# A table's copies queued behind a weight load instead of behind a write of activations (one-core decoder trunk)

## The chip, the cores and the metric

One core of a Trainium2 chip runs the whole program. The metric is device time in microseconds (us) of one execution, as the median of several.

## The reference

Two layers work on 256 tokens of width 1024. Each layer mixes tokens (short convolution, sliding-window attention, chunked spatial gating) and then runs PEER, a retrieval over 16384 single-neuron experts. All the parts that matter here are in PEER:

```python
q = (t @ w_pq).reshape(T, PEER_HEADS, 2, PEER_HALF)
s = jnp.einsum('thpk,hpnk->thpn', q, sub_keys)
top_s, top_i = lax.top_k(s, PEER_TOPK)                 # 16 of 128 keys, twice per head
...                                                    # best 16 of the 256 pairs
gate = jax.nn.softmax(best_s, axis=-1)
u = expert_down[experts]
act = jax.nn.gelu(jnp.einsum('td,thkd->thk', t, u), approximate=False)
vv = expert_up[experts]
return jnp.einsum('thk,thkd->td', gate * act, vv)
```

Besides, each layer needs 48 columns of modulation, `silu(c) @ w_ada + b_ada`.

## The kernel before, in words

The kernel computes PEER densely: all 16384 activations for all 256 tokens, in 128 chunks of 128 experts (the **down stage**, function `experts`), each multiplied by its gate (zero for experts that a token didn't choose), and then all of the up projection (the **up stage**, function `combine`). One part of the up projection is done sparsely instead: for the second 128 tokens and the last `WIDE[layer]` output columns (256 in layer 0, 384 in layer 1) the chosen rows alone are fetched and added.

For that the down stage builds a table in the chip's memory, `rows[layer]` (L100), one row for each expert. A row has `WIDE` columns of the up matrix and 128 columns with that expert's ungated activations of the second 128 tokens. `act` (L944) fills it, once for each pair of chunks: ScalarE (ACT) computes the ungated activations (L949) into the tile `ungated`, of which there is one buffer, and sends it (L950) from its own queue; SyncE (SP) copies the up matrix's columns from memory to memory (L951, 256 KB a pair in layer 0, 384 KB in layer 1). The activations' piece has 129 columns and begins one column early, at `WIDE - 1`, in the last column that the copy writes too. So the copy, which stands second in the text, has to wait until the piece has landed, and then sets that column right. In the up stage, GpSimd fetches 128 sets of rows by index (L1007) and VectorE adds them (L1013, L1018).

The other work of the down stage: each chunk of weights (128 by 1024, 512 KB) is loaded by SP into one of five `raw` buffers (`dma_ahead`, L170; the load is L175), at most five chunks ahead of the chunk that is split next (`cast_step`, L207). ACT makes its rounded half `hi` (L232), VectorE (DVE) the rest `lo` (L225); TensorE (PE) then does three products for each of eight slices (L303 to L305) into a `ch` bank, of which there are two, each for a pair of chunks. ACT applies the gelu (L959, L962) and the ungated gelu (L949). From about the middle on, PE also makes gates from one-hot tiles (L918 to L932), which DVE and ACT multiply in (L939, L942).

In layer 0 the stream of loads in the down stage is mixed with 40 chunks of `w_ada` (`mix`, L291). These don't go to PE: DVE reduces each of them by itself with two instructions (L193), and then the buffer is free. Layer 1's down stage has none of them.

The order of instructions on each engine outside the stretches marked as manual (the up stage and the two bridges are manual) is set by a planner that follows an estimate of each instruction's time (`schedule_with_timeline_sim=True`, L1244). Each engine and each queue then runs its instructions in that order; an instruction that waits holds up those behind it.

Of the kernel before, what the change touches and what calls it, by code (L numbers as in the profile page):

```python
# [9 lines left out]
F32 = mybir.dt.float32  # L10
# [3 lines left out]
AF = mybir.ActivationFunctionType  # L14
# [3 lines left out]
P = 128  # L18
# [3 lines left out]
D = 1024  # L22
# [22 lines left out]
WIDE = (256, 384)  # L45
# [13 lines left out]
def hybrid_trunk(ctx: ExitStack, tc: tile.TileContext, x_in, c_in, vec_in, w_ada, w_in, w_out, w_pq,  # L59
                 keys, down, up, rel_bias, sgu_w, sgu_b, out):  # L60
    nc = tc.nc
    consts = ctx.enter_context(tc.tile_pool(name="consts", bufs=1))
    stream = ctx.enter_context(tc.tile_pool(name="stream", bufs=1))
    work = ctx.enter_context(tc.tile_pool(name="work", bufs=1))
# [35 lines left out]
    rows = {n: dram.tile([P * P, WIDE[n] + P], F32, name=f"rows{n}") for n in range(DEPTH) if SPARSE[n]}  # L100
# [62 lines left out]
    class Src:  # L163
        c = cact
# [149 lines left out]
    def bank(tag, bufs):  # L314
        return psum.tile([P, 512], F32, name=tag, tag=tag, bufs=bufs)
# [590 lines left out]
    def experts(layer, rest):  # L906
# [37 lines left out]
        def act(pair, ps, tdone):  # L944
            tmp = gelu(pair, ps, tdone)
            if SPARSE[layer]:
                i = 2 * pair
                ungated = work.tile([P, 2, P + 1], F32, name="ungated", tag="ungated", bufs=1)
                nc.scalar.activation(ungated, ps.rearrange("p (i t) -> p i t", i=2)[:, :, P - 1:], AF.Gelu)  # L949
                nc.scalar.dma_start(rows[layer].rearrange("(j i) c -> i j c", i=P)[:, i:i + 2, WIDE[layer] - 1:], ungated)  # L950
                nc.sync.dma_start(rows[layer][i * P:(i + 2) * P, :WIDE[layer]],  # L951
                                  up[layer, i:i + 2, :, D - WIDE[layer]:].rearrange("j i c -> (j i) c"))
            return tmp

        def gelu(pair, ps, tdone):
            i = 2 * pair
            v = ps.rearrange("p (i t) -> p i t", i=2)
            if tdone < S:
                nc.scalar.activation(arena[:, i:i + 2, tdone:], v[:, :, tdone:], AF.Gelu)  # L959
            if tdone:  # L960
                tmp = work.tile([P, 2, S], F32, name="gt", tag="gt", bufs=1)
                nc.scalar.activation(tmp[:, :, :tdone], v[:, :, :tdone], AF.Gelu)  # L962
                return tmp
            return None
# [148 lines left out]
        for i in range(128):  # L1113
            pair, j = divmod(i, 2)
            if j == 0:
                ps = bank("ch", 2)
# [28 lines left out]
            if j == 1:  # L1145
                tdone = 4 * gdone
                pend = (pair, act(pair, ps, tdone), tdone)
# [101 lines left out]
```

## Time and profile before

| | us |
|---|---|
| median of 3 runs | 1821.18 |
| lowest and highest run | 1818.62, 1821.8 |
| the profiled execution, its own time | 1817.31 |
| its span, first to last instruction | 1815.6 |

One execution is profiled. Busy times are by engine; "PEld" is TensorE's weight load, "SPq" and "ACTq" are the queues in which SyncE and ScalarE issue transfers. A wait names the instruction that was released, what released it, the total in us, how often, and the longest. An instruction's row ends with the idle time of its engine ahead of it and what ended that, in square brackets.

### The profile page before, as it was taken

Reading aid. Unit: us, or ns where it says so; the run is one execution under the profiler, and the core shown is the slowest. Engines: PE = TensorE matmul, PEld = TensorE weight load, DVE = VectorE, ACT = ScalarE, POOL = GpSimd, SP = SyncE. Lnnn points to the kernel's source line nnn. Section 1 sums busy time; section 2 is a strip of 40 time slices with the busy share of each in tenths; the row PEclk is TensorE's granted clock in tenths of the full one; section 3 lists DMA queues with packets and bytes.
Section 4 is the critical chain, followed back from the end, with each engine's and each line's share of the span. In section 5 each row is a group of like instructions: output and inputs, shape, how many; then the busy total and the mean of one; then the engine's idle time right before and its main releaser. Section 6 shows DMA issues by size and latency. Waiting matters only on the chain. (4 is left out here: it accounts for less than half of the span.)

```text
span 1815.6 us, 34513 instructions
## 1 busy us (share of the span) xinstructions
PE 1746.4 (96%) x12504; PEld 1608.5 (89%) x12504; DVE 1517.4 (84%) x3465; ACT 915.4 (50%) x1419; POOL 921.3 (51%) x826
## 2 busy tenths in 40 slices
PE   7999998999999999999999999999999999999998
PEld 6789998998889988888889999999999998888886
DVE  5868988888888789999996689957778877999998
ACT  2445454454444554445456665555555546444543
POOL 1000102577889456666720002037999982777672
PEclk9999999999999999999999999999999999999999
DMA  9965687887787699999974456888787778999995
GB/s 369 323 232 165 228 276 262 285 264 257 255 260 243 228 317 329 338 337 343 342 258 152 139 175 191 269 269 274 250 257 225 248 240 292 361 346 343 358 350 206
DMA packets 189868, 492.97 MB, mean 272 GB/s; under 512 B 19521, under 2 KB 85441, under 8 KB 188546
## 3 DMA queue, kind: packets, MB, share of 16 engines
q1 hardware_dynamic: 134752, 405.33, 66.7%
q0 software_dynamic: 19984, 68.44, 10.2%
q10 hardware_dynamic: 34962, 17.01, 3.3%
q8 instruction: 98, 1.61, 0.4%
q14 instruction: 72, 0.59, 0.1%
HBM read 470.64 MB, written 62.00 MB: 293 GB/s over the span
## 5 line engine op out<-in xcount | busy, mean ns | idle before, releaser
L232 ACT CAST hi<-raw 128x1024 fp32r<-128x1024 f32 x538 | 563.9, 1050 | 609.7 <-PE ch L305 250.6
L225 DVE TENSOR_TENSOR lo<-raw,hi 128x1024 fp32r<-128x1024 f32 x538 | 660.1, 1229 | 124.2 <-ACT hi L232 120.1
L304 PE MATMUL ch<-hh,lo 128*128 128x256 f32 x2336 | 659.1, 282 | 17.3 <-DVE lo L225 17.1
L303 PE MATMUL ch<-hh,hi 128*128 128x256 f32 x2336 | 664.0, 284 | 3.1 <-ACT ungated L949 3.1
L305 PE MATMUL ch<-hh,hi 128*128 128x256 f32 x2336 | 655.3, 281 | 0.0
L918 POOL TENSOR_SCALAR oh<-iota,picks 128x128 f16<-128x128 f16 x512 | 509.8, 1013 | 236.4 <-DVE picks L848 127.2
L1007 POOL DMA_INDIRECT arena<-rows,arena x256 | 371.0, 1449 | 222.7 <-DVE arena L1018 103.4
L304 PEld LDWEIGHTS ch<-hh,lo 128*128 128x128 f32 x2336 | 444.8, 190 | 22.4 <-DVE lo L225 22.1
L303 PEld LDWEIGHTS ch<-hh,hi 128*128 128x128 f32 x2336 | 444.5, 190 | 4.2 <-ACT ungated L949 3.7
L305 PEld LDWEIGHTS ch<-hh,hi 128*128 128x128 f32 x2336 | 444.5, 190 | 0.0
L1027 PE MATMUL acc<-hi,hh 128*128 128x512 f32 (+2 forms) x1920 | 419.6, 359 | 3.8 <-DVE hh L985 2.6
L1027 PEld LDWEIGHTS acc<-hi,hh 128*128 128x128 f32 x1920 | 339.3, 188 | 50.5 <-DVE hh L985 7.0
L1027 PE MATMUL acc<-lo,hh 128*128 128x512 f32 x960 | 231.1, 361 | 3.3 <-DVE lo L225 2.8
L1027 PEld LDWEIGHTS acc<-lo,hh 128*128 128x128 f32 x960 | 172.5, 188 | 28.6 <-DVE lo L225 4.8
L1018 DVE SCALAR_TENSOR_TENSOR arena<-arena 128x256 f32<-128x256 f32 (+1 forms) x254 | 140.3, 552 | 9.1
L942 ACT ACTIVATE arena<-g 128x240 f32<-128x240 f32 (+35 forms) x128 | 41.6, 325 | 120.7 <-DVE arena L939 105.6
L779 POOL CAST arena<-arena 128x512 f16<-128x512 uint32 x32 | 27.2, 864 | 147.6 <-DVE arena L768 116.4
L923 DVE TENSOR_TENSOR oh<-oh,parts 128x512 f16<-128x512 f16 x256 | 101.4, 437 | 0.0
L193 DVE SCALAR_TENSOR_TENSOR raw<-raw,acc 128x512 f32<-128x512 f32 x80 | 51.9, 684 | 54.2 <-DMA raw<-in_w_ada 54.2
L931 PE MATMUL g<-oh 128*128 128x128 f16 x512 | 75.8, 222 | 17.5 <-POOL oh L918 8.8
L1013 DVE SCALAR_TENSOR_TENSOR arena<-arena,chosen,ident 128x128 f32<-128x128 f32 x256 | 89.2, 349 | 1.7 <-DMA arena<-rows,arena 1.7
L921 DVE TENSOR_TENSOR oh<-iota,parts 128x512 f16<-128x512 f16 x128 | 56.7, 444 | 28.8 <-POOL oh L918 16.0
(231 smaller groups left out, 1788.7 us busy)
## 6 DMA issues: line engine op xcount, KB each, us to landing
raw<-in_down SPq DMA_DIRECT2D x256, 512.0 KB
raw<-in_up SPq DMA_DIRECT2D x256, 512.0 KB
raw<-in_w_ada SPq DMA_DIRECT2D x96, 512.0 KB
rows<-in_up SPq DMA_DIRECT2D x64, 384.0 KB
rows<-ungated ACTq DMA_DIRECT2D x128, 129.0 KB
raw<-in_w_pq SPq DMA_DIRECT2D x32, 512.0 KB
rows<-in_up SPq DMA_DIRECT2D x64, 256.0 KB
raw<-in_w_in SPq DMA_DIRECT2D x26, 512.0 KB
```

The source lines that it names most:

```text
L225: nc.vector.tensor_sub(lo, raw, hi.bitcast(F32))
L232: nc.scalar.copy(hi, raw)
L303: nc.tensor.matmul(dst, hi[:, cols], k[0], start=start, stop=False, **kw)
L304: nc.tensor.matmul(dst, lo[:, cols], k[0], start=False, stop=False, **kw)
L305: nc.tensor.matmul(dst, hi[:, cols], k[1], start=False, stop=stop, **kw)
L918: nc.gpsimd.tensor_scalar(oh[:, i, :], iota, picks[:, t:t + 1], None, op0=OP.is_equal)
L923: nc.vector.tensor_tensor(og[j], on, wide(1 + j), op=OP.mult)
L931: nc.tensor.matmul(dst, oh[:, i, :], og[0][:, i // 2, :, i % 2], start=True, stop=False)
L1007: nc.gpsimd.indirect_dma_start(out=ring[:, k % RING, :], out_offset=None, in_=rows[layer][:, :], in_offset=bass.IndirectOffsetOnAxis(ap=wh ...
L1013: nc.vector.scalar_tensor_tensor(v[:, wide:], v[:, wide:], chosen[:, 1, k:k + 1], ident, op0=OP.mult, op1=OP.mult, accum_out=w8[:, k:k + 1])
L1018: nc.vector.scalar_tensor_tensor(total, v[:, :wide], w8[:, k:k + 1], total, op0=OP.mult, op1=OP.add)
L1027: nc.tensor.matmul(acc[piece][:, :hi - lo], w[:, t * P:(t + 1) * P], u[:, lo:hi], start=piece not in opened, stop=last, skip_group_check=True)
```

## The change

The activations' piece loses the shared column: it has 128 columns and begins at `WIDE`. The copy then touches no column that another transfer writes. Without that wait the planner would be free to put it anywhere; the new call pins it, in SP's order of issue alone, behind the instruction last traced on SP, which is a load of weights (L175). It doesn't wait for that load to land.

```diff
@@ -945,11 +945,12 @@
             tmp = gelu(pair, ps, tdone)
             if SPARSE[layer]:
                 i = 2 * pair
-                ungated = work.tile([P, 2, P + 1], F32, name="ungated", tag="ungated", bufs=1)
-                nc.scalar.activation(ungated, ps.rearrange("p (i t) -> p i t", i=2)[:, :, P - 1:], AF.Gelu)
-                nc.scalar.dma_start(rows[layer].rearrange("(j i) c -> i j c", i=P)[:, i:i + 2, WIDE[layer] - 1:], ungated)
-                nc.sync.dma_start(rows[layer][i * P:(i + 2) * P, :WIDE[layer]],
-                                  up[layer, i:i + 2, :, D - WIDE[layer]:].rearrange("j i c -> (j i) c"))
+                ungated = work.tile([P, 2, P], F32, name="ungated", tag="ungated", bufs=1)
+                nc.scalar.activation(ungated, ps.rearrange("p (i t) -> p i t", i=2)[:, :, P:], AF.Gelu)
+                nc.scalar.dma_start(rows[layer].rearrange("(j i) c -> i j c", i=P)[:, i:i + 2, WIDE[layer]:], ungated)
+                tc.keep_in_program_order(nc.sync.dma_start(
+                    rows[layer][i * P:(i + 2) * P, :WIDE[layer]],
+                    up[layer, i:i + 2, :, D - WIDE[layer]:].rearrange("j i c -> (j i) c")))
             return tmp
```

## Rows read from the trace of the kernel before

**Rows 1.** The page, its first lines: the span and the busiest engine.

```profile
span 1815.6 us, 34513 instructions
PE 1746.4 (96%) x12504; PEld 1608.5 (89%) x12504; DVE 1517.4 (84%) x3465; ACT 915.4 (50%) x1419; POOL 921.3 (51%) x826
```

**Rows 2.** Table by stretch: the two down stages, then two stretches of low clock.

```profile
core 0: us, PE busy (x) PEld busy (x) DVE busy (x) ACT busy (x) POOL busy (x), PEclk, DMA share, GB/s
195.00:632.00 437.00, 406.09 (x3554) 395.09 (x3553) 361.36 (x860) 212.91 (x374) 250.48 (x264) 0.98 0.79 258
1110.00:1508.00 398.00, 390.60 (x3563) 384.07 (x3563) 316.54 (x690) 214.22 (x375) 271.99 (x264) 1.00 0.80 250
275.20:278.60 3.40, 3.40 (x18) 3.40 (x18) 3.13 (x10) 0.98 (x1) 0.00 (x0) 0.50 0.91 269
323.00:326.40 3.40, 3.40 (x18) 3.40 (x17) 3.40 (x7) 1.43 (x2) 0.00 (x0) 0.50 0.70 206
...
```

**Rows 3.** Waits of SP's queue, stretch 195 to 632 us, then 1110 to 1508 us.

```profile
SPq L951 <- DMA rows<-ungated: 150.8, 54, 8.0
...
SPq L951 <- DMA rows<-ungated: 224.2, 63, 6.1
```

**Rows 4.** Waits of DVE, ACT and PE in layer 0's down stage, 195 to 632 us.

```profile
DVE raw L193 <- DMA raw<-in_w_ada: 54.2, 28, 4.9
...
ACT hi L232 <- DMA raw<-in_down: 14.0, 4, 5.0
ACT ungated L949 <- DMA rows<-ungated: 8.2, 9, 2.6
...
PE ch L304 <- DVE lo L225: 14.9, 16, 2.1
PE g L931 <- DVE oh L923: 7.2, 5, 2.1
```

**Rows 5.** Waits of ACT in layer 1's down stage, 1110 to 1508 us.

```profile
ACT hi L232 <- PE ch L305: 128.1, 97, 3.4
ACT ungated L949 <- DMA rows<-ungated: 30.0, 17, 3.2
```

**Rows 6.** Instructions in order, PE, 264 to 344 us: where it stood.

```profile
267.09 0.39 PE L303 MATMUL ch<-hh,hi 128*128 128x256 f32 x1 [0.97 <-ACT ungated L949]
274.92 0.39 PE L304 MATMUL ch<-hh,lo 128*128 128x256 f32 x1 [2.10 <-DVE lo L225]
283.31 0.39 PE L304 MATMUL ch<-hh,lo 128*128 128x256 f32 x1 [0.84 <-DVE lo L225]
321.73 0.38 PE L304 MATMUL ch<-hh,lo 128*128 128x256 f32 x1 [1.87 <-DVE lo L225]
337.96 0.22 PE L931 MATMUL g<-oh 128*128 128x128 f16 x1 [0.44 <-POOL oh L918]
```

**Rows 7.** Instructions in order, SP's queue, 260 to 276 us, and DVE's at 272 us.

```profile
264.57 0.50 SPq L951 DMA_DIRECT2D rows<-in_up  x1
265.12 0.60 SPq L175 DMA_DIRECT2D raw<-in_w_ada  x1
...
272.42 0.69 DVE L193 SCALAR_TENSOR_TENSOR raw<-raw,acc 128x512 f32<-128x512 f32 x1 [4.33 <-DMA raw<-in_w_ada]
```

**Rows 8.** Instructions in order, SP, ACT and DVE, 411 to 419 us.

```profile
411.07 0.33 SPq L175 DMA_DIRECT2D raw<-in_w_ada  x1
412.95 0.33 SPq L175 DMA_DIRECT2D raw<-in_down  x1
417.45 0.50 SPq L951 DMA_DIRECT2D rows<-in_up  x1
...
412.11 0.37 ACTq L950 DMA_DIRECT2D rows<-ungated  x1
...
416.48 0.69 DVE L193 SCALAR_TENSOR_TENSOR raw<-raw,acc 128x512 f32<-128x512 f32 x1 [3.33 <-DMA raw<-in_w_ada]
```

**Rows 9.** Instructions of line L949: count, least, median and most ns.

```profile
L949 ACT ACTIVATE ungated<-ch x128: 374/388/407, 195.6 to 1506.2; 128x258 f32<-128x258 f32 x128
```

**Rows 10.** The page, DMA queues of SP and ACT: packets, MB, share of 16 engines.

```profile
q1 hardware_dynamic: 134752, 405.33, 66.7%
q10 hardware_dynamic: 34962, 17.01, 3.3%
```

**Rows 11.** ACT's longest stop for the piece in layer 1, and that stretch's table.

```profile
1182.61 0.39 ACT L949 ACTIVATE ungated<-ch 128x258 f32<-128x258 f32 x1 [3.17 <-DMA rows<-ungated]
...
1162.00:1190.00 28.00, 28.00 (x247) 27.91 (x246) 23.76 (x47) 14.13 (x22) 3.60 (x2) 1.00 0.85 263
```

## The prediction

> **What bounds the kernel now.** I read the page's busy line first [rows 1]: PE is busy for 1746.4 of 1815.6 us, so at most 69 us of the span is time in which PE stands, wherever it lies. The change touches the two down stages, so the table by stretch comes next [rows 2]. Both stages do the same products (3554 and 3563 matmuls), but layer 0 takes 437.00 us and layer 1 takes 398.00. In layer 0 PE stands 437.00 - 406.09 = 30.9 us and has a granted clock of 0.98, which costs another 437 x 0.02 = 8.7 us. In layer 1 it stands 7.4 us at full clock. So this change can give at most about 40 us in layer 0 and 7 us in layer 1.
>
> Then the waits. SP stands at the copy for the activations' piece to land: 150.8 us in layer 0 and 224.2 us in layer 1, some 3 us for each copy [rows 3]. That is the wait that goes. What it is worth has to be read from those who wait for the loads behind it. In layer 1 ACT's list has no wait for a load at all [rows 5]: 224 us of SP's standing cost PE nothing there, because five buffers cover it. In layer 0 DVE waits 54.2 us in 28 pieces for `w_ada` chunks, ACT 14.0 us in 4 pieces for expert chunks [rows 4], and PE's own waits are for DVE (`lo` and the one-hots), which are queued behind those reductions.
>
> So the question is which of layer 0's late loads are late because of the copy. Two samples show both kinds. In the first [rows 7] the copy goes at 264.57 and the `w_ada` load right behind it at 265.12; DVE then waits 4.33 us and PE 2.10 us, after which its granted clock is 0.50 (1.2 of 2.4 GHz) for 3.4 us [rows 2, 6]. In the second [rows 8] the load goes at 411.07, ahead of the copy (417.45); DVE nevertheless reaches its reduction 2.1 us after the issue, and waits 3.33 us until 416.48. There the planner put the reduction too early for a load that takes 5.4 us; the copy has no part in it.
>
> **The change, part by part.**
>
> *SP's wait is gone.* Nothing else on SP replaces it: a copy then costs its issue only. The loads behind it (one or two in each pair) go when a buffer is free. Of layer 0's PE stops, five belong to loads issued behind a copy that had stood: 0.97 + 2.10 + 0.84 + 1.87 + 0.44 = 6.2 us [rows 6]. Two of them were followed by a spell at half clock of 3.4 us, which costs 1.7 us each [rows 2]: 3.4 us more. The sum is 9.6 us. I don't take all of it, since where the copy's delay goes, the other kind of wait remains: DVE waits 54.2 / 28 = 1.9 us for each of them on average, against 4.33 us in the sample. I take two thirds, 6.4 us. The lower bound of this term is 0 and the upper bound layer 0's whole 40 us (all `w_ada` waits gone); the five stops are the nearest rows.
>
> *Layer 1:* between 0 and the 7.4 us that PE stands. PE has no wait on a load there, so I take 0.
>
> *One column less on ACT:* 256 instead of 258 elements in an instruction of 388 ns [rows 9], 128 times. At 388 / 258 = 1.5 ns for each element at most that is 3 ns x 128 = 0.4 us of an engine that is busy half of the time. It is hidden by PE; without that cover it would be 0.4 us.
>
> *The activations' write, 129 to 128 columns:* ACT's queue takes 3.3% of the DMA engines, 0.033 x 1815.6 / 128 = 0.47 us for each piece [rows 10]. Starting on another column may make it cheaper or dearer; no row shows it. I bound it by -0.47 and +0.47 us of a landing of 5.3 us (412.11 to 417.45, [rows 8]) and take 0: ACT waits for that landing, PE doesn't.
>
> *The copies go earlier,* by the 3 us that they stood. They are pinned behind the load last traced, so they move past no load, and the bytes are the same. SP's queue took 0.667 x 1815.6 = 1211 us for 405 MB [rows 10], 3.0 us per MB; a copy is 0.78 us of all engines in layer 0, 1.17 us in layer 1. What it now meets is the activations' piece, which it used to follow. That is a rival below. POOL's first fetch of rows needs all copies; they land earlier than before, so nothing waits longer.
>
> *A new plan.* The planner sees other times, so the order on DVE and ACT in both down stages will differ in places. No row shows its price. The nearest bound is what the present order costs where no `w_ada` interferes, layer 1's 7.4 us; I take 0 and keep -4 and +5 us for the range.
>
> The sum: 1817.3 - 6.4 = 1810.9 us for the profiled execution. That one lies 3.9 us below the median of the runs shown, 1821.2; against the median it is 1814.8 us. A measurement of this kernel can tell about 0.2%, 3.6 us, from no change.
>
> **The rivals.**
>
> *No change (0.28).* Layer 0's waits are those of rows 8, made by the order on DVE: a reduction stands about 2 us behind its load's issue, and the load takes 5 us or more, with or without a copy. When the five stops shrink, DVE reaches the next reduction earlier and waits there instead. For it: 28 waits, far more than five, and layer 1, where SP's standing is worth nothing. Against it: the waits of over 4 us have a copy just ahead. The time is 1821 us. It would also be the outcome if the change did not do what it says and SP still stood at the copy for something else.
>
> A rule of the Trainium skill points the same way. "DMA: Bandwidth & Descriptors", section "Issuing engines are not separate DMA queues", says (in my words) that transfers issued by different engines share the same 16 DMA engines, and that an issuing queue of one's own saves only the time of issuing. By that rule, freeing SP alone gives no transfer time back, and the sum would be 0; the trace has it so in layer 1.
>
> *Slower (0.20): the copy gets in the way of the activations' piece.* Until now the copy was issued only when the piece had landed; now the copy's bytes are in the engines when the piece is sent. The piece lands later by up to the copy's 0.78 or 1.17 us. Its tile has one buffer, so ACT stands at the next L949, and behind that in its queue are the casts that PE needs. ACT already waits 17 times, 30.0 us in all, in layer 1 [rows 5]. The place where it decides: ACT stood 3.17 us and PE was busy 28.00 of 28.00 us around it [rows 11], so a stop of some 3 us is still covered. Beyond that each us reaches PE. If all 17 waits went over by 1.17 us, that would be 20 us, and 9 x 0.78 = 7 us in layer 0. Half of the sum is likelier, as the waits are of different length: +13, less the 6.4 gained, +7 us, 1828 us.
>
> On this another rule of that page of the Trainium skill speaks against the change: its section "Queues, rings and completion order", has a transfer's completion signal land only after every earlier write of the same DMA engine, across queues. The row agrees so far as 0.47 us of data takes 5.3 us to be reported [rows 8, 10].
>
> *A large gain (0.10).* If loads that go without delay are also spread more evenly, each takes less than 5.4 us, and half of the 54.2 us that DVE waits goes [rows 4], with it half of layer 0's 40 us: -20 us, 1801 us. Against it: DMA is at 0.79 in this stage anyway.
>
> **How the numbers follow.** The forecast, 5 to 12 us faster, has a chance of 0.42; no change 0.28, slower 0.20, large gain 0.10. Faster by over 0.2%: 0.42 + 0.10 = 0.52; within 0.2%: 0.28; slower: 0.20. The range goes from the large gain's near half, 1803, to the slower rival's 1828; what lies outside is about half of each of these two, 0.15. The likeliest case alone has 1809 to 1817.
>
> **What would show it.** Right: no row of SP's line for the copy waiting for the piece; layer 0's stretch shorter than 437 us by 5 to 10, with fewer and shorter waits for loads (below 54.2 and 14.0 us) and fewer spells at half clock; layer 1's stretch within 2 us. The rival "no change" shows as the same 50 us of DVE waiting for `w_ada` in spite of a free SP. The slower rival shows as ACT's waits for the piece well above 30.0 us in layer 1, with PE waiting for `hi` or L949. The forecast is wrong if PE's standing in layer 0 stays at 31 us, or if the new order brings PE a stop that stands in no row here.

## The result, and the profile after

| | before, us | after, us |
|---|---|---|
| median (4 runs each) | 1819.9 | 1802.61 |
| lowest and highest | 1814.51, 1821.8 | 1801.73, 1804.13 |
| the profiled execution, its own time | 1817.31 | 1804.13 |
| its span | 1815.6 | 1802.4 |

The ratio is 0.9911, 95% interval 0.9887 to 0.9934: 0.9% faster, or 16 us of 1819.9, where 6.4 us were forecast. The likeliest case was right in sign and too small; the median stands 0.4 us under the low end of the range (1803).

The first view is the table by stretch of the kernel after, cut as in [rows 2] (from 0.6 us ahead of the first ungated gelu of layer 0 to 3.8 us behind the first product of the up stage, and in layer 1 from 1.0 us ahead to 4.7 us behind); then a spell at half clock around PE's longest stop (3.53 us), and 3.4 us that follow its longest but one (2.30 us).

```profile
core 0: us, PE busy (x) PEld busy (x) DVE busy (x) ACT busy (x) POOL busy (x), PEclk, DMA share, GB/s
196.20:623.90 427.70, 399.51 (x3553) 388.22 (x3552) 362.43 (x864) 212.15 (x374) 239.64 (x264) 0.99 0.83 266
1099.40:1495.80 396.40, 389.08 (x3564) 383.27 (x3563) 317.86 (x698) 213.28 (x375) 270.81 (x264) 1.00 0.82 255
299.20:306.00 6.80, 5.95 (x28) 5.95 (x29) 6.38 (x16) 2.27 (x4) 0.11 (x1) 0.50 0.81 248
389.00:392.40 3.40, 3.40 (x34) 3.26 (x34) 3.40 (x8) 1.86 (x4) 2.15 (x1) 1.00 0.80 246
```

Layer 0's stretch went from 437.0 to 427.7 us, layer 1's from 398.0 to 396.4. In layer 0 PE stands 427.70 - 399.51 = 28.2 us against 30.9, so only 2.7 us of the 9.3 are standing. The other 6.6 us are PE's busy time, 406.09 to 399.51 for the same products, mostly because less of it ran at the lower clock (0.99 granted for the stretch against 0.98). These are two single executions; how far they stand for the kernels is taken up below.

The waits of layer 0's stretch answer to [rows 3, 4]: SP's queue, then DVE, ACT and PE.

```profile
SPq L175 <- DVE lo L225: 138.6, 65, 3.7
SPq L175 <- DMA raw<-in_w_ada: 48.3, 26, 3.7
```

```profile
DVE raw L193 <- DMA raw<-in_w_ada: 47.8, 30, 4.2
...
ACT ungated L949 <- DMA rows<-ungated: 20.3, 16, 3.7
...
PE ch L304 <- DVE lo L225: 13.7, 14, 2.3
PE ch L303 <- ACT ungated L949: 5.8, 3, 3.5
...
PE g L931 <- DVE oh L923: 3.8, 5, 1.1
```

SP no longer waits for the piece; it waits for buffers. ACT's 14.0 us of waits for expert chunks are gone. But DVE's waits for `w_ada` are almost what they were: 47.8 us in 30 pieces, against 54.2 in 28. One of them, in the order of time on SP's queue, DVE and PE:

```profile
379.45 0.33 SPq L175 DMA_DIRECT2D raw<-in_w_ada  x1
380.59 0.33 SPq L175 DMA_DIRECT2D raw<-in_down  x1
380.97 0.51 SPq L951 DMA_DIRECT2D rows<-in_up  x1
...
384.96 0.69 DVE L193 SCALAR_TENSOR_TENSOR raw<-raw,acc 128x512 f32<-128x512 f32 x1 [4.23 <-DMA raw<-in_w_ada]
...
388.74 0.38 PE L304 MATMUL ch<-hh,lo 128*128 128x256 f32 x1 [2.30 <-DVE lo L225]
```

The copy now stands right behind a load and holds nothing up. DVE came to its reduction 1.3 us after the load's issue and waited until 384.96, 5.5 us after it. PE paid 2.30 us. This is the pattern of [rows 8], and the change leaves it alone. Both samples are from the low end. By the timelines of SP and DVE, DVE reaches the 40 reductions of this stage 3.9 us (median) behind their loads' issue before the change and 4.1 us after it, which is still less than the 5.1 us (median) that a `w_ada` load takes to land.

### The profile page after: what moved, and what is told of

Read it like the earlier page. It is cut to its first block, busy times and chain, and to the rows that moved or that the text cites. A ratio compares the mean times of both kernels' runs of the same rounds, so it can differ in the third digit from the quotient of the medians.

```text
span 1802.4 us, 34404 instructions
## 1 busy us (share of the span) xinstructions
PE 1736.8 (96%) x12504; PEld 1599.5 (89%) x12504; DVE 1515.8 (84%) x3465; ACT 913.6 (51%) x1419; POOL 907.5 (50%) x826
## 3 DMA queue, kind: packets, MB, share of 16 engines
q1 hardware_dynamic: 134752, 405.33, 67.4%
## 5 line engine op out<-in xcount | busy, mean ns | idle before, releaser
L918 POOL TENSOR_SCALAR oh<-iota,picks 128x128 f16<-128x128 f16 x512 | 498.4, 991 | 235.4 <-DVE arena L833 67.4
L1028 PE MATMUL acc<-hi,hh 128*128 128x512 f32 (+2 forms) x1920 | 419.5, 359 | 2.8 <-DVE hh L986 2.4
L193 DVE SCALAR_TENSOR_TENSOR raw<-raw,acc 128x512 f32<-128x512 f32 x80 | 51.8, 683 | 47.8 <-DMA raw<-in_w_ada 47.8
```

The costliest lines, as they stand in the source:

```text
L918: nc.gpsimd.tensor_scalar(oh[:, i, :], iota, picks[:, t:t + 1], None, op0=OP.is_equal)
L1028: nc.tensor.matmul(acc[piece][:, :hi - lo], w[:, t * P:(t + 1) * P], u[:, lo:hi], start=piece not in opened, stop=last, skip_group_check=True)
```

## The experiments

All ratios are to the kernel before, run on the same chip. "Layer 0" is the stretch cut as above, in the one profiled execution; "stands" is that stretch less PE's busy time, "clock" its granted clock.

| kernel | ratio, 95% interval | layer 0, us | PE stands, us | clock |
|---|---|---|---|---|
| before | 1 | 437.0 | 30.9 | 0.98 |
| before_again | 0.9986 (0.9965 to 1.0006) | 438.8 | 31.2 | 0.97 |
| wait_kept | 0.9976 (0.9954 to 0.9999) | 429.7 | 31.0 | 0.99 |
| free_layer1 | 0.9974 (0.9954 to 0.9994) | 429.3 | 28.5 | 0.99 |
| free_layer0 | 0.9936 (0.9910 to 0.9961) | 419.3 | 24.5 | 1.00 |
| after | 0.9911 (0.9887 to 0.9934) | 427.7 | 28.2 | 0.99 |
| after_again | 0.9894 (0.9859 to 0.9930) | 428.7 | 31.8 | 1.00 |
| order_only | 0.9914 (0.9881 to 0.9946) | 419.5 | 23.4 | 0.99 |
| no_pin | 1.0483 (1.0455 to 1.0511) | 410.6 | 17.5 | 1.00 |
| before_no_ada | 1.0027 (1.0013 to 1.0041) | 398.3 | 6.5 | 1.00 |
| after_no_ada | 1.0006 (0.9993 to 1.0020) | 394.0 | 6.9 | 1.00 |
| before_reduce_late | 0.9892 (0.9867 to 0.9917) | 416.6 | 20.1 | 0.98 |
| after_reduce_late | 0.9799 (0.9770 to 0.9827) | 400.1 | 10.0 | 1.00 |
| order_reduce_late | 0.9794 (0.9775 to 0.9814) | 399.5 | 9.6 | 1.00 |

**The two kernels again.**

> The kernel before, a second time, for the spread. All theories: a ratio of 1.000. If the profile repeats, layer 0's down stage (from the first ungated gelu to the first product of the up stage) is 433 us again, layer 1's 392 us, and layer 0's has some six spells at half clock and 31 us in which PE stands. If a second profile differs by several us in a stage, so much of the 13 us between the two profiles is spread and not the change.

> The changed kernel, a second time. A ratio of 0.991 again (0.989 to 0.993). Layer 0's down stage 423 us against 433, half of the spells at half clock (three), PE standing some 28 us. If the spells are chance, this profile may have five or six and layer 0's stage is then nearer to 428 us.

Both ratios repeat. The profiles repeat in length (438.8 and 428.7 us), and here PE's standing hardly differs: 31.2 and 31.8 us. What differs is PE's busy time, 407.6 against 396.9 us, with a granted clock of 0.97 against 1.00. But neither execution is a typical one. That of after_again is the slowest of its six (1807.4 us, median 1798.2), and that of before_again has the lowest granted clock of its twelve (0.991 over the whole run, median 0.995). So this pair alone doesn't show that the gain is time at the lower clock.

**The wait kept, the column gone.** The wait for the landing stays by an explicit dependency instead of the shared column. In both down stages the orders on SP, ACT, DVE and PE are those of before.

```diff
-                tc.keep_in_program_order(nc.sync.dma_start(rows[layer][i * P:(i + 2) * P, :WIDE[layer]], ...))
+                copy = nc.sync.dma_start(rows[layer][i * P:(i + 2) * P, :WIDE[layer]], ...)
+                tc.add_manual_dep(copy.ins, piece.ins.name,
+                                  mybir.DependencyInfo(mybir.DependencyClass.Sync, mybir.DependencyReason.DATA))
```

> The shared column goes as in the change, but SP's wait for the piece stays, by an explicit dependency. Theory (SP's wait while the program runs is what cost): the time of the kernel before, ratio 1.000, SP stands some 375 us at the copy again. Rival (the piece of 128 columns, starting where the copy ends, is cheaper to write and lands sooner): ratio 0.991 as after the change, and a landing well below 5 us. Rival (the planner's order): its order of SP's queue is almost that of before, so 1.000 too.

0.9976, where 1.000 was expected: about a quarter of the gain, from the narrower piece alone. By itself this is barely clear of the spread (the kernel before came out at 0.9986 the second time), but two more comparisons below have the same 0.2 to 0.3%. Waits of SP in layer 0 and layer 1, as in [rows 3]:

```profile
SPq L951 <- DMA rows<-ungated: 130.4, 54, 6.1
...
SPq L951 <- DMA rows<-ungated: 202.3, 63, 6.1
```

SP stands 332.7 us instead of 375.0, some 0.3 us less for each copy: the piece lands that much sooner. The rest of the gain needs SP's wait to go. This profiled execution (1807.8 us) is one of the kernel's faster ones (median 1812.2), so its 429.7 us flatters it.

**The order kept, the wait gone.** The same edit with a dependency of order alone (`DependencyClass.NoSync`): the copy stands behind the piece's issue in the plan and waits for nothing of it.

> The copy is planned behind the issue of the piece, as an order alone: no wait for the landing. Theory (SP's wait is what cost): close to the changed kernel, ratio 0.990 to 0.994, with SP hardly standing at the copy. Rival (the gain is this particular new order of the work on DVE, ACT and PE): the order here is again a different one, so the ratio may be anywhere from 0.990 to 1.005, and DVE's waits for w_ada differ from the 48 us of after.

0.9914, the changed kernel's ratio, with quite another order on PE and DVE, and SP no longer stands at the copy. So the gain goes with SP's wait and not with one particular plan. No run has the order of before without the wait, so a share of the new orders isn't excluded; but two orders that differ this much give the same ratio.

**One layer at a time.** The pin in one layer, the explicit wait in the other (`if layer == 0`, or 1).

> The change in layer 0 alone; in layer 1 the copy waits for the piece as before. Theory (the late loads matter where w_ada is reduced): nearly the whole gain, ratio 0.988 to 0.993, with SP standing some 210 us at the copy in layer 1 for nothing. Rival (each layer gives its part, since SP stands 150 us in one and 215 in the other): ratio 0.995 to 0.996.

> The change in layer 1 alone; in layer 0 the copy waits for the piece. Theory: next to nothing beyond the kernel with the wait kept in both layers (0.998), ratio 0.996 to 1.000; layer 0's down stage 425 to 434 us. Rival (each layer gives its part): 0.994 to 0.995.

Freeing layer 1 adds nothing to the narrower piece: 0.9974 against 0.9976, though SP stood 202.3 us there. Freeing layer 0 has 0.9936, just short of the 0.988 to 0.993 that I had expected; its interval overlaps those of the kernel after. In layer 0 its order on every engine is that of the changed kernel, and yet its profile has 419.3 us where that one's two have 427.7 and 428.7. So one execution's stretch varies by 9 us with the same order, and single profiles don't settle shares of a few us.

**The reductions late.** Each `w_ada` reduction of the down stage is pinned in DVE's order behind what stands before it in the text, with the change and without it:

```diff
-            nc.vector.scalar_tensor_tensor(v, v, 1.0, c, op0=OP.mult, op1=OP.mult, accum_out=m[:, col:col + 1])
+            red = nc.vector.scalar_tensor_tensor(v, v, 1.0, c, op0=OP.mult, op1=OP.mult, accum_out=m[:, col:col + 1])
+            if len(sides) > 1:
+                tc.keep_in_program_order(red)
```

> The changed kernel, and each w_ada reduction in the down stage is pinned in DVE's order behind what stands before it in the text, so four loads' worth of work lies between its load's issue and the reduction. Theory (what is left in layer 0 are reductions that the planner puts some 2 us behind the issue of a load that takes 5): DVE's wait for w_ada falls from 48 to below 15 us, PE stands below 20 us in layer 0's down stage instead of 28 to 32, and the ratio to the kernel before is 0.980 to 0.986. Rival (PE's stops come from the sum of DVE's work, not from the order): the wait on DVE moves to other rows and the ratio stays at 0.989 to 0.993.

> The kernel before with the same pin of the reductions, so that the copy's wait stands alone. Theory (the copy's wait costs because loads that are needed at once come late): with the reductions late, most of the cost of SP's wait goes as well; ratio to before 0.980 to 0.990, and at most 0.4% slower than the changed kernel with the same pin. Rival (SP's wait costs by itself, 1%): 1% slower than that kernel.

With the change, the table and DVE's wait are:

```profile
195.80:595.90 400.10, 390.12 (x3553) 382.85 (x3552) 365.43 (x864) 214.59 (x374) 262.06 (x264) 1.00 0.88 284
```

```profile
DVE raw L193 <- DMA raw<-in_w_ada: 2.2, 2, 1.8
```

DVE's wait is 2.2 us instead of 47.8, PE stands 10.0 us instead of 28.2, and the ratio is 0.9799, twice the gain of the change. What was left in layer 0 was mostly the order of the reductions.

The expectation for the second kernel failed. I had SP's wait cost at most 0.4% once the reductions are late; the two kernels are 0.9892 - 0.9799 = 0.93% apart. The narrower piece is in that, too; without its 0.2% the wait costs some 0.7%. Its waits in layer 0 (SP, ACT, PE):

```profile
SPq L953 <- DMA rows<-ungated: 210.0, 61, 7.9
...
ACT hi L234 <- DMA raw<-in_down: 61.1, 28, 5.6
...
PE ch L306 <- DVE lo L227: 13.0, 7, 5.8
```

Now ACT waits for expert chunks, 61.1 us in 28 pieces, a wait that the kernel with both edits doesn't have. A late load hurts whatever reads it first. It isn't the reductions alone.

**No `w_ada` in the down stage.** All of layer 0's 40 chunks are moved to the up stage, which gets longer by 45 us and more; only the distance between the two kernels counts.

```diff
-            dn = mix(dn, ada(0, [5]) + ada(1, range(4)), 4, 112)
-            ups = mix(ups, ada(1, [4, 5]), 6, 120)
+            ups = mix(ups, ada(0, [5]) + ada(1, range(6)), 6, 120)
```

> The kernel before, with no w_ada chunks in layer 0's down stage; they are all reduced in its up stage. Theory (SP's wait costs where 2.6 loads a pair have to pass in 5.6 us, and nothing where two do, as in layer 1): layer 0's down stage is as long as layer 1's, 388 to 396 us, with SP standing 200 us and more at the copy; the up stage of layer 0 grows by some 40 loads. The total is of no matter here, only the distance to the next kernel.

> The changed kernel, with no w_ada chunks in layer 0's down stage. Theory: at most 0.3% faster than the last kernel (the piece's share) and layer 0's down stage within 3 us of that one's. Rival (SP's wait costs by itself, wherever it stands): 0.8 to 1% faster than the last kernel, as with the w_ada chunks.

```profile
195.70:594.00 398.30, 391.78 (x3554) 386.52 (x3553) 317.49 (x693) 213.08 (x374) 271.79 (x264) 1.00 0.71 231
```

```profile
SPq L950 <- DMA rows<-ungated: 219.5, 62, 5.1
```

Without the change SP stands 219.5 us at the copy in this stretch, and PE stands 6.5 us: as in layer 1. The two kernels differ by 1.0027 - 1.0006 = 0.21%, what the narrower piece had given by itself. Their stages are 4.3 us apart (398.3 and 394.0), where I had expected at most 3. So SP's wait costs 0.4 to 0.8% (0.9976 less 0.9936 to 0.9894) where 168 loads have to pass in the stage, and nothing that can be told from the spread where 128 do. This edit takes the 40 reductions off DVE as well as the 40 loads off SP; that the loads matter without the early reductions is what before_reduce_late shows. The same five buffers then hold the loads of 1.9 pairs of chunks (2.6 loads a pair) instead of 2.5.

**No pin.**

```diff
-                tc.keep_in_program_order(nc.sync.dma_start(
+                (nc.sync.dma_start(
```

> The changed kernel without the pin: nothing holds the copies, and the planner puts those of layer 0 among the first loads of the program and those of layer 1 among the loads of the mixing stages. Theory: 64 copies of some 0.8 us of all DMA engines each, 50 us, now lie in the first 100 us, where DMA is busy at 0.93: the stretch before the down stage grows from 196 us by 30 to 50 us, the down stage of layer 0 gets shorter by 10 to 20 us without them, and the ratio to before is 1.005 to 1.02. Rival (copies are hidden wherever they stand): 0.985 to 0.990.

4.8% slower, twice and more what I had expected, because I put only layer 0's copies at the front. The planner puts layer 1's there too. The table of the stretch before the down stage (196 us in the kernel after):

```profile
0.00:317.00 317.00, 201.15 (x1147) 175.39 (x1148) 150.55 (x441) 86.87 (x176) 14.04 (x26) 0.82 0.85 295
```

It is 121 us longer. All copies together are 42 MB, at the 3.0 us per MB of [rows 10] 126 us. The down stage of layer 0 without them is 410.6 us. The pin, or the wait before it, is what keeps 42 MB under cover.

**Order and late reductions together.**

> The copy ordered behind the piece's issue without a wait, and the w_ada reductions pinned late. Theory (copies issued around the piece's issue rather than 5 us ahead of it make no difference): ratio 0.977 to 0.983, the same as with the changed kernel and late reductions (0.980). Rival (copies ahead of the piece make it land later and ACT wait): ACT's waits for the piece fall from 28 us to below 15 and the ratio is 0.974 to 0.978.

The same as after_reduce_late within the intervals. ACT's wait for the piece did fall in layer 0 (8.6 us against 22.9), though it rose in layer 1 (11.3 against 5.0), and it was worth nothing.

## Why the prediction was right, and where it was off

*SP's wait is gone:* shown, and it carries most of the gain (wait_kept against order_only and the kernel after). The step that failed is the size of this term. I put it at 6.4 us; the ratios give (0.9976 - 0.9911) to (0.9976 - 0.9894) of 1816, 12 to 15 us, and 7 us for layer 0 freed alone (0.9976 - 0.9936), each ratio good to some 4 us. The price came from five stops that all lie between 264 and 344 us of a stage of 437 us, and the last of them (0.44 us) was ended by POOL and not by a late load. Of their 9.6 us I took two thirds "since ... the other kind of wait remains". The other kind does remain (47.8 of 54.2 us), and the cut was too deep all the same.

Whether the gain is standing or clock, the profiles don't settle. Before against after it looks like clock alone (PE stands 30.9 and 31.2 us before, 28.2 and 31.8 after). But wait_kept and free_layer1, which keep SP's wait in layer 0, have 0.99 there, as the first profile of the kernel after has, and both profiles of the kernel after are the slowest of their runs. The granted clock of every run says more. On one chip its median is 0.995 for the kernel before (24 runs) and for wait_kept (12), 0.997 for order_only (7) and 0.998 for after_again (6). 0.002 to 0.003 of 1816 us is 4 to 5 us, at most, of the 16 to 19 us that these two kernels gain. Another 4 us is the piece. The rest, 8 to 10 us, is most likely PE's standing, which is 23.4 us in order_only and 24.5 in free_layer0, 6 to 8 us less than before, in one execution each. So both parts of the price, standing and half clock, were right in kind. Which stops bring such a spell isn't settled: the stop of 2.30 us at 388.74 is followed by full clock, a stop of 2.10 us in [rows 2, 6] by half. The link from loads that come in time to the clock is argued from the totals, not shown stop by stop.

*Layer 1, 0:* right. Its stretch went by 1.6 us, and free_layer1 shows nothing beyond the piece.

*The piece, 0:* mis-sized. It lands about 0.3 us sooner, inside the bound of 0.47, but gives some 0.2%, 4 us (wait_kept, free_layer1 and the two kernels without `w_ada` agree on it). I had given that bound to ACT and SP alone and none of it to PE.

*The copies go earlier by 3 us:* wrong in size. They are pinned behind a load that is five chunks ahead, and stand before the piece that they used to follow, in layer 0 by 5.6 us in the median (at 380.97 here, where the piece of the same pair goes at 389.84). It cost nothing: order_only has them at about the piece's issue, with the same ratio.

*The rival "slower"* fell, but its mechanism shows in one place of the first profile (ACT's queue, SP's queue, ACT, PE):

```profile
285.51 0.37 ACTq L950 DMA_DIRECT2D rows<-ungated  x1
...
286.42 0.50 SPq L951 DMA_DIRECT2D rows<-in_up  x1
...
292.97 0.38 ACT L949 ACTIVATE ungated<-ch 128x256 f32<-128x256 f32 x1 [3.61 <-DMA rows<-ungated]
...
300.05 0.58 PE L303 MATMUL ch<-hh,hi 128*128 128x256 f32 x1 [3.53 <-ACT ungated L949]
```

A copy went 0.91 us behind the piece, and the piece held ACT up until 7.5 us after it was sent. ACT stood 3.61 us for it and then worked on with no stop above 0.52 us until it released PE from its longest stop, beside 6.8 us at half clock. I had taken a stop of some 3 us to be covered, from one place of layer 1 [rows 11]; here nearly all of it came out at PE. That the copy made the piece late is not shown. The second profile has no such place (ACT's longest wait for the piece is 1.5 us in layer 0). In all, ACT's wait for the piece in layer 1 went from 30.0 to 4.4 us in one profile and to 23.9 in the other; in layer 0 from 8.2 to 20.3 and 10.7. The median landing of the piece after is 4.5 us, with the copies issued some 5 us ahead of it. It is 4.8 and 4.9 us in before_reduce_late and before_no_ada, where the copies wait behind a piece of 129 columns, and 5.0 us in order_reduce_late, where they go at about the piece's issue. The rule of the Trainium skill that was quoted against the change ("DMA: Bandwidth & Descriptors", "Queues, rings and completion order") may hold, but no run here shows by itself that copies ahead of the piece delay its report.

*The rival "no change"* had its mechanism right, though 2 us was a sample from the low end and 3.9 us is the median: the reductions' order is worth as much as the change (1 to 0.9892 without it, 0.9911 to 0.9799 with it). It did not cancel the gain. The rule of the Trainium skill that an issuing queue saves issue time only ("DMA: Bandwidth & Descriptors", "Issuing engines are not separate DMA queues") would have the sum at 0. The runs agree in layer 1 and in the kernels without `w_ada` there, and not in layer 0 with it: SP's queue moved the same 405.33 MB, but fewer loads came late (DVE and ACT wait 68.2 and 67.2 us for loads in layer 0's two profiles before, 47.8 and 50.6 us in those after).

*A large gain* through evenly spread loads: it needed the reductions' order as well.

## What to carry to other kernels

A queue that stands 150 us in one stage may cost 0.4 to 0.8% and one that stands 224 us in another nothing: look at who waits for the transfers behind it, stage by stage, and count how many loads its buffers have to cover in that stage. Where a planner orders work by its own estimate of landings, an operation that waits for almost every load is a sign of a too early place; pinning it a few loads later was worth as much here as freeing the queue. A transfer that nothing holds goes wherever a planner likes, so replace a wait by an order, not by nothing.

## What was not expected

With the narrower piece PE itself is mostly a little less busy. In layer 1's stretch, where no load is waited for, PE is busy for 390.6 us before [rows 2], for 390.0, 389.9 and 390.2 us in the other three kernels with the 129-column piece, and for 387.8 to 389.1 in seven with 128 columns. Two of the seven (after and free_layer0) even have 3.4 us at half clock in that stretch, which costs 1.7 us; all the others have full clock. Three more with 128 columns and a different order there (order_only, no_pin and order_reduce_late) have 389.2 to 390.2, so it isn't the width alone. No run here shows the cause.
